# A pointwise product computed as two groups of two column blocks, with neighbouring steps moved inside it

## The chip, the cores and the metric

The kernel runs on one core of one Trainium2 chip. The metric is device time in microseconds of one execution, lower is better; times are given as the median of several runs. All arithmetic is float32 in and out. The engines named below are PE (matrix products), DVE and ACT (elementwise work), POOL (a few small powers) and SP, whose queue issues the loads.

## The reference

One layer of a hybrid block on 256 tokens of width 4096: attention heads (A) and a convolution module (C) work on the same normed input, both are gated, joined and projected; then a gated embedding is added and the result is normed. Cut to what matters here:

```python
xn = rms_norm(h, norm_in_g)
proj = xn @ w_in                       # q, k, v, z_a, a_c, g_c, z_c, 2048 columns each
y_a = chunked_attention(q, k, v, rel_table)
y_a = rms_norm(y_a, attn_out_g) * silu(z_a)
# convolution module
u = a_c * sigmoid(g_c)
u = causal_depthwise_conv(u, w_dw) + b_dw
u = silu(layer_norm(u, conv_ln_g, conv_ln_b))
y_c = u @ w_pw + b_pw                  # the pointwise product, 2048 x 2048
y_c = rms_norm(y_c, conv_out_g) * silu(z_c)
h = h + concatenate([y_a, y_c]) @ w_out
gate = sigmoid(rms_norm(h, ple_norm_g) @ w_ple_gate + b_ple_gate)
h = h + gate * (p @ w_ple)
return rms_norm(h, final_g)
```

## The kernel before

**Products.** The 256 tokens are two halves of 128 rows; an output column block is 512 wide (NB). Every float32 operand is split into a high and a low part (wh, wl for weights), and a product of two blocks is three matmuls of 128 x 512: high times wh, low times wh, high times wl. A weight tile of 128 x 1024 is loaded by SP into `wt` (5 buffers), cast to `wh` by ACT (L304, 5 buffers), and `wl` is the difference, made by DVE (L321, 5 buffers). `prepare` issues load and cast of the next unit of a plan one step ahead.

There are two forms of product. `product` (matmuls at L255) computes one column block: two accumulators (one per half of the rows) out of four PSUM banks, so that consecutive blocks alternate between two pairs of banks. `mixed_product` (matmuls at L449) computes two column blocks at once in all four banks, over 16 (or 8) pairs of 128-row weight blocks. A pair of an order is plain (8 products, 24 matmuls) or starred, which means that it is done with 7 products (21 matmuls) on sums of blocks: the weights' sums are made on DVE (L324, L327) and the inputs' sums, the combinations, lie ready in `xS`. Four further banks (acc_P) hold helper sums in such a group. Orders are strings of pair numbers; two of them matter here:

```python
    dense = units("1 0* 3 2* 5 4* 6* 7 8* 9 10* 11 12* 14* 13 15")
    delayed = units("1 3 5 7 0* 9 2* 11 4* 13 6* 15 8* 10 12 14")
```

In the first and the last pair of a `mixed_product` the matmuls go bank by bank, in between block by block.

**What runs beside the products.** Two queues of small steps are emptied inside the products: `later` (taps of the convolution, the layer norm's steps) by `fill(n)`, n steps per unit, and `closing` (the steps of heads), one step per `fill`. A scheduler then fixes one order of instructions on each engine; ACT, DVE and SP work through theirs in order.

**Around the change.** The last `heads` call queues the layer norm (`layer_norm_swish`) and computes the last v product. Of the layer norm's tail, for each of four column blocks, `swish` scales (DVE, L843) and applies the swish (ACT, L844), and `split` makes the high part (ACT, L854) and the low part (DVE, L855) of `uS`, the pointwise product's input. Then `fill(1e9)` and `finish_steps` empty both queues: the rest of the tail, v's evacuation (ACT, L953), the last heads' values (PE, L961 to L963, evacuated by ACT at L965), the squares of y_a (ACT, L564) and `r_a`. Then the scratch pool is closed and another opened; four `product` calls (32 units) compute the pointwise product, DVE adds the bias row (L1028, rows loaded at L1010) and ACT sums squares. Behind them in the program stand the eight combinations of the input (`combine_again`, six DVE instructions and one ACT copy each), whose results the four gate groups (`gated`, each a `mixed_product` over `w_in`) read. `gate_order` gives the first gate group the order `delayed` and the other three `dense`.

Of the kernel before, what the change touches and what calls it, by code (L numbers as in the profile page):

```python
# [16 lines left out]
P = 128  # L17
# [14 lines left out]
def hybrid_block(  # L32
# [40 lines left out]
    def pool(name, bufs, stack=ctx, side=0, **kw):  # L73
        return stack.enter_context(tc.tile_pool(name=name, bufs=bufs, side=sides[side], **kw))
# [83 lines left out]
    def big_tile(pool=None):  # L158
        return (pool or big).tile([P, 4, 2, T], F32R, tag="big", name="big_t")
# [45 lines left out]
    def finish_steps():  # L205
        while closing:
            step()

    def fill(n):
        step()  # L210
        credit[0] += n
        while later and credit[0] > 0:
            item = later.popleft()
            weight, item = item if isinstance(item, tuple) else (1, item)
            credit[0] -= weight
            item()
        if not later:
            credit[0] = 0
# [42 lines left out]
    def units(text):  # L261

        return [(int(u.rstrip("*")), u.endswith("*")) for u in text.split()]
# [4 lines left out]
    delayed = units("1 3 5 7 0* 9 2* 11 4* 13 6* 15 8* 10 12 14")  # L268
    early = units("1 3 5 0* 7 9 2* 11 4* 13 6* 15 8* 12 10* 14")
    late = units("1 3 5 7 9 11 13 15 0* 2 4* 6 8* 10* 12 14")  # L270

    plan, prepared = deque(), []

# [40 lines left out]
    def plan_product(w, col, kblocks, first=0):  # L314
        plan.extend((w, col, None, k0, "one") for k0 in range(first, kblocks, KC))

    def plan_pairs(w, col, apart, order):
        plan.extend((w, col, apart, pair, "seven" if seven else "pair") for pair, seven in order)
# [57 lines left out]
    def sum_rows():  # L376
        return [spool.tile([P, NB], F32, tag="row", name="comb", bufs=3) for _ in range(2)]
# [22 lines left out]
    def combine_again(dst, at, t, i, rows):  # L400

        a, s = rows
        nc.vector.tensor_tensor(
            a.rearrange("q (i t) -> q i t", t=T), t[:, i : i + 2, 0, :].bitcast(F32),
            t[:, i : i + 2, 1, :].bitcast(F32), ALU.add,
        )
        combined_parts(dst, at, s, a[:, :T], a[:, T : T + P], a[:, T + P :], 1.0)

    def comb_tile(combs):

        if len(combs) < D // NB // 2 - 1:
            combs.append(big_tile(more))
        else:
            combs.append(spool.tile([P, 4, 2, T], F32R, tag="comb", name="comb_t", bufs=1))
# [147 lines left out]
    def square_sum(dst, src):  # L562
        junk = spool.tile([P, NB], mybir.dt.bfloat16, tag="s", name="junk", bufs=1 if more_scratch else 2)
        nc.scalar.activation(junk, src, AF.Square, accum_out=dst)  # L564

    def rstd_of(partial, n, name):
        r = cpool.tile([P, partial.shape[1]], F32, name=name)
        nc.vector.tensor_reduce(r, partial, AX.X, ALU.add)
        rsqrt(r, r, n)
        return r  # L570
# [86 lines left out]
    AG_ORDER, QK_ORDER = early, early  # L657

    def gate_order(c0):
        return dense if c0 else delayed  # L660

    plan_product(w_in0, o_g, KD, FIRST)
    plan_product(w_in0, o_a, KD)
    for g in range(n_g):
# [1 line left out]
            plan_pairs(w_in0, o_a + (g + 1) * NB, o_g - o_a, AG_ORDER)  # L666
        plan_pairs(w_in0, o_q + g * NB, o_k - o_q, QK_ORDER)
        plan_product(w_in0, o_v + g * NB, KD)
    for c in range(CW // NB):
        plan_product(w_pw0, c * NB, KCW)  # L670
    for o_z in (o_za, o_zc):
        for c0 in range(0, AW // NB, 2):
            plan_pairs(w_in0, o_z + c0 * NB, NB, gate_order(o_z != o_za or c0))
# [103 lines left out]
    def layer_norm_swish():  # L777

        add = nc.vector.tensor_tensor
        st = {}  # L780

        def scratch(name):
            t = more.tile([P, 2, 4, T], F32, tag="big", name=name)
            return [t[:, j] for j in range(2)]

        def fold(s):
            add(s[:, :2, :], s[:, :2, :], s[:, 2:, :], ALU.add)
            add(s[:, 0, :], s[:, 0, :], s[:, 1, :], ALU.add)
            return s[:, 0, :]

        def stat(key, m, scale=1.0):
            st[key] = cpool.tile([P, T], F32, tag="ln_stat", name=key)
            nc.scalar.activation(st[key], m, AF.Identity, scale=scale)

        def mean(s):

            m = tmp_psum()
            nc.tensor.matmul(m[:, :T], mean_w, fold(s), start=True, stop=True)
            stat("mu", m[:, :T])

        def total(c):
            if c == 0:
                st["s"] = act.tile([P, 4, T], F32, tag="act", name="lnsum")
                add(st["s"], conv[0], conv[1], ALU.add)
            elif c > 1:
                add(st["s"], st["s"], conv[c], ALU.add)

        def center(c, i):
            cv = conv[c]
            nc.vector.tensor_tensor(cv[:, i, :], cv[:, i, :], st["mu"], ALU.subtract)  # L810

        def square(c):
            if c == 0:
                st["q"], st["t"] = scratch("sq")
            s = st["t"] if c else st["q"]
            nc.scalar.activation(s, conv[c], AF.Square)
            if c:
                add(st["q"], st["q"], s, ALU.add)

        def variance(s):  # L820

            s = fold(s)
            m = tmp_psum()
            for h in range(NH):
                nc.tensor.matmul(
                    m[:, h : h + 1], s[:, h * P : (h + 1) * P], mean_w[:, :1],
                    start=True, stop=True,
                )
            st["r"] = cpool.tile([P, NH], F32, name="r_ln")
            rsqrt(st["r"], m[:, :NH], 1)  # L830

        def spread(s):

            m = tmp_psum()
            for h in range(NH):
                d = s[:, 0, h * P : (h + 1) * P]
                nc.vector.tensor_scalar(d, ident, st["r"][:, h : h + 1], None, ALU.mult)
                nc.tensor.matmul(m[:, h * P : (h + 1) * P], mean_w, d, start=True, stop=True)
            stat("rs", m[:, :T], float(CW))

        def swish(c, i):
            cv, b = conv[c], 4 * c + i
            nc.vector.tensor_tensor(cv[:, i, :], cv[:, i, :], st["rs"], ALU.mult)  # L843
            nc.scalar.activation(  # L844
                cv[:, i, :], cv[:, i, :], AF.Silu,
                scale=ln_g[:, b : b + 1], bias=ln_b[:, b : b + 1],
            )

        def split(c, i):
            if i == 0:  # L850
                assert more is not None
                uS.append(big_tile(more))
            hi, lo = uS[c][:, i, 0, :], uS[c][:, i, 1, :]
            nc.scalar.copy(hi, conv[c][:, i, :])  # L854
            nc.vector.tensor_tensor(lo, conv[c][:, i, :], hi.bitcast(F32), ALU.subtract)  # L855

        n = len(conv)
        rest = [lambda: None] * 4
        later.extend(partial(total, c) for c in range(n))
        later.append(lambda: mean(st["s"]))  # L860
        later.extend(rest)

        def second():
            for c in range(n):
                later.extend(partial(center, c, i) for i in range(4))
                later.append(partial(square, c))
            later.append(lambda: variance(st["q"]))
            later.extend(rest)
            later.append(lambda: spread(st["t"]))
            later.extend(rest)  # L870
            for c in range(n):
                later.extend(partial(swish, c, i) for i in range(4))
            for c in range(n):
                later.extend(partial(split, c, i) for i in range(4))

        return second
# [127 lines left out]
    closing.append(lambda: r_as.append(rstd_of(ssq_a, AW, "r_a")))  # L1004


    def broadcast_row(src, n0, n):

        t = spool.tile([P, n], F32, tag="row", name="row", bufs=3)
        nc.sync.dma_start(  # L1010
            t, bass.AP(tensor=src.tensor, offset=src.offset + n0, ap=[[0, P], [1, n]])
        )
        return t

    fill(1e9)
    finish_steps()
    r_a, = r_as
    first_scratch.close()
    spool = upool = pool("lpool", 2, side=1)
    more_scratch.append(1)  # L1020
    y_c = []
    ssq_c = cpool.tile([P, NH, CW // NB], F32, name="ssq_c")
    for c in range(CW // NB):
        row = broadcast_row(b_pw, c * NB, NB)
        acc = product(w_pw0, c * NB, uS, KCW)
        y = act.tile([P, NH, NB], F32, tag="act", name="y_c")
        for h in range(NH):
            nc.vector.tensor_tensor(y[:, h, :], acc[h], row, ALU.add)  # L1028
            square_sum(ssq_c[:, h, c : c + 1], y[:, h, :])
        y_c.append(y)  # L1030
    r_c = rstd_of(ssq_c, CW, "r_c")


    xS = []
    for c in range(D // NB):
        if c % 2 == 0:
            comb_tile(xS)
        combine_again(xS[c // 2], 2 * (c % 2), xT[c], 0, sum_rows())

    def gated(ys, c0, col, r_y, order):  # L1040

# [196 lines left out]
```

## Time and profile before

| what | value |
|---|---|
| median of 3 runs | 2045.38 us (2044.98 to 2045.83) |
| the profiled execution | 2045.17 us, span 2043.4 us |
| mean granted clock of PE | 0.996 |
| layer norm's last scalings on DVE begin | 888.27 us |
| last matmul of the last v product begins | 897.87 us |
| pointwise product on PE | 901.07 to 995.85 us |
| first gate group on PE | 995.85 to 1079.50 us |
| second, third, fourth gate group | 81.60 us each |

Times inside the span are counted from its start. A row of the profile names a line of the kernel, an engine, an operation, the tile written and the tiles read; in brackets stands the idle time of the engine just before and what ended it. The span is the time from the first to the last instruction; the execution's own time is 1.8 us more.

### The profile page before, as it was taken

The numbers are of one execution on the slowest core, as the hardware profiler recorded it, in microseconds if no ns is written. First come the engines' busy times: TensorE is split into PE (matmuls) and PEld (weight loads), VectorE is DVE, ScalarE is ACT, GpSimd is POOL, SyncE is SP. The second block draws the span as 40 slices with busy tenths as digits, with TensorE's granted clock in tenths as the row PEclk, the third lists the DMA queues.
The fourth block names the chain that finished last, engine by engine and source line by source line (L and its number), as shares of the span: only waits on it lengthen the run. The fifth ranks groups of instructions, "written<-read, shape, count | busy, mean of one in ns | idle before, by whom it ended". The sixth has DMA issues, their size and how long they took to land.

```text
span 2043.4 us, 26018 instructions
## 1 busy us (share of the span) xinstructions
PE 2018.3 (99%) x9103; PEld 1668.4 (82%) x9103; DVE 1801.0 (88%) x2124; ACT 1373.3 (67%) x2033; POOL 14.7 (1%) x23
## 2 busy tenths in 40 slices
PE   9999999999999999999999999999999999999997
PEld 6888888888888888878888888888888888888886
DVE  7589997999799988975889999999999998999954
ACT  7477798778977797774555656675565675665543
POOL 0000000000000000000000000000000000000010
PEclk9999999999999999999999999999999999999999
DMA  8646665666566665746565665666656655666774
GB/s 303 186 165 207 191 208 171 213 195 208 165 198 203 196 196 175 217 153 214 171 227 173 214 208 192 239 227 198 214 191 221 206 191 191 211 229 206 230 221 144
DMA packets 170333, 412.29 MB, mean 202 GB/s; under 512 B 13006, under 2 KB 16222, under 8 KB 170202
## 3 DMA queue, kind: packets, MB, share of 16 engines
q1 hardware_dynamic: 169914, 410.11, 62.1%
q8 instruction: 71, 1.16, 0.2%
q10 hardware_dynamic: 288, 0.52, 0.1%
q14 instruction: 60, 0.49, 0.1%
HBM read 406.39 MB, written 4.19 MB: 201 GB/s over the span
## 4 chain that ended last, share of the span: by engine, by line
PE 95%; DVE 2%; ACT 1%; issue 1%; DMA 1%; ACTq 0%; POOLq 0%; POOL 0%; DVEq 0%
PE acc L449 55%; PE acc L255 22%; PE acc_P L449 15%; DVE wl L321 1%; PE tmp_ps L179 1%; DMA wt<-in_w_in_dram 0%; PE tmp_ps L888 0%; PE tmp_ps L924 0%; PE tmp_ps L946 0%; ACT big_t L854 0%; ACT wh L304 0%; ACT junk L564 0%; PE tmp_ps L134 0%; DMA pin<-in_p_dram 0%; PE tmp_ps L923 0%
## 5 line engine op out<-in xcount | busy, mean ns | idle before, releaser
L321 DVE TENSOR_TENSOR wl<-wt,wh 128x1024 fp32r<-128x1024 f32 x961 | 1091.8, 1156 | 143.0 <-ACT wh L304 119.4
L449 PE MATMUL acc<-wh,big_t 128*128 128x512 f32 x3410 | 1052.2, 390 | 1.3 <-ACT big_t L165 0.7
L304 ACT CAST wh<-wt 128x1024 fp32r<-128x1024 f32 x727 | 698.5, 981 | 324.1 <-PE acc L449 106.1
L449 PEld LDWEIGHTS acc<-wh,big_t 128*128 128x128 f32 x3410 | 638.4, 188 | 133.5 <-ACT big_t L165 1.2
L449 PE MATMUL acc<-wl,big_t 128*128 128x512 f32 x1705 | 662.8, 389 | 0.4 <-DVE wl L321 0.4
L255 PE MATMUL acc<-wh,big_t 128*128 128x512 f32 x1248 | 393.8, 397 | 7.1 <-ACT wh L304 5.7
L449 PEld LDWEIGHTS acc<-wl,big_t 128*128 128x128 f32 x1705 | 320.0, 188 | 67.5 <-DVE wl L321 0.8
L255 PEld LDWEIGHTS acc<-wh,big_t 128*128 128x128 f32 x1248 | 232.5, 189 | 55.8 <-ACT wh L304 6.5
L449 PE MATMUL acc_P<-wh,big_t 128*128 128x512 f32 x852 | 262.2, 389 | 0.3 <-ACT wh L491 0.3
L255 PE MATMUL acc<-wl,big_t 128*128 128x512 f32 x624 | 244.1, 392 | 0.1
L327 DVE TENSOR_TENSOR wt<-wt 128x512 f32<-128x512 f32 x234 | 224.2, 958 | 7.5
L491 ACT CAST wh<-wt 128x1024 fp32r<-128x1024 f32 x117 | 123.3, 1054 | 158.1 <-DVE wt L327 129.2
L716 ACT ACTIVATE prod<-uT,dw 128x255 f32<-128x255 f32 (+14 forms) x480 | 200.7, 489 | 2.7 <-DVE cv L723 2.5
L449 PEld LDWEIGHTS acc_P<-wh,big_t 128*128 128x128 f32 x852 | 159.7, 188 | 33.6 <-ACT wh L491 0.7
L488 ACT CAST wh<-wt 128x1024 fp32r<-128x1024 f32 x117 | 123.3, 1054 | 81.5 <-DVE wt L327 76.4
L449 PE MATMUL acc_P<-wl,big_t 128*128 128x512 f32 x426 | 165.3, 389 | 0.0
L723 DVE TENSOR_TENSOR cv<-cv,prod 128x1020 f32<-128x1020 f32 (+14 forms) x120 | 138.7, 1156 | 21.2 <-ACT prod L716 21.0
L255 PEld LDWEIGHTS acc<-wl,big_t 128*128 128x128 f32 x624 | 117.5, 189 | 26.5 <-DVE wl L321 1.3
L449 PEld LDWEIGHTS acc_P<-wl,big_t 128*128 128x128 f32 x426 | 79.9, 188 | 17.0 <-DVE wl L321 0.2
L324 DVE TENSOR_TENSOR wt<-wt 128x512 f32<-128x512 f32 x117 | 80.2, 685 | 0.2 <-DMA wt<-in_w_ple_gate_dram 0.2
L564 ACT ACTIVATE junk<-hc 128x512 bf16<-128x512 f32 x32 | 20.2, 630 | 20.9 <-DVE hc L1095 8.4
L165 ACT ACTIVATE big_t<-tmp_ps,prm 128x256 fp32r<-128x256 f32 x64 | 27.5, 473 | 4.6 <-DVE big_t L166 4.6
(190 smaller groups left out, 937.9 us busy)
## 6 DMA issues: line engine op xcount, KB each, us to landing
wt<-in_w_in_dram SPq DMA_DIRECT2D x447, 512.0 KB, 4.6
wt<-in_w_out_dram SPq DMA_DIRECT2D x128, 512.0 KB, 4.6
wt<-in_w_ple_gate_dram SPq DMA_DIRECT2D x128, 512.0 KB, 4.4
wt<-in_w_pw_dram SPq DMA_DIRECT2D x32, 512.0 KB, 4.6
hc<-in_x_dram SPq DMA_DIRECT2D x8, 512.0 KB, 5.4
wt<-in_w_ple_dram SPq DMA_DIRECT2D x8, 512.0 KB, 5.5
out_dram<-hc SPq DMA_DIRECT2D x16, 256.0 KB, 2.7
xin<-in_x_dram SPq DMA_DIRECT2D x7, 512.0 KB, 8.0
```

The lines of the kernel that those rows point to most:

```text
L165: nc.scalar.activation(hi, src, AF.Identity, scale=scale),
L179: nc.tensor.transpose(pt[:, i * T + h * P : i * T + (h + 1) * P], src[:, h, b * P : (b + 1) * P], ident,)
L255: nc.tensor.matmul(acc, a, b[:, k, :], start=kb == 0 and kind == 0, stop=kb == kblocks - 1 and kind == 2,)
L304: chain(nc.scalar.copy(highs[k][:, :n], wt[:, :n]))
L321: return chain(nc.vector.tensor_tensor(wl, wt, wh.bitcast(F32), ALU.subtract))
L324: return chain(nc.vector.tensor_tensor(out, a, b, ALU.add))
L327: return chain(nc.vector.tensor_tensor(out, a, b, ALU.subtract))
L449: nc.tensor.matmul(banks[name], a, b, start=name not in begun, stop=final and ends[name] == n and kind == 2,)
L488: chain(nc.scalar.copy(ah, w0))
L491: chain(nc.scalar.copy(bh, w1))
L716: chain(nc.scalar.activation(dst[:, i, : T - n], uT[:, i, : T - n], AF.Identity, scale=dw[:, b, TAPS - 1 - n : TAPS - n], bias=0.0 if n el ...
L723: chain(nc.vector.tensor_tensor(cv[:, :, n:], cv[:, :, n:], made[n][:, :, : T - n], ALU.add))
```

## The change

Three things are rearranged; what is computed stays the same.

- The pointwise product becomes two `mixed_product` calls, each of two column blocks in four banks, over eight plain pairs (`plain8`). Its loads are 128 rows of 1024 columns in place of two blocks of 128 x 512.
- `swish` and `split` are queued column block by column block. Before the product only the steps up to column block 0 are emptied; the other 24 are emptied inside the first group, 4 per pair, and so are v's evacuation, the values, the squares, `r_a` and the change of scratch pools, which are now `closing` steps.
- The combinations become `later` steps of the second group, one per pair. All four gate groups take the order `dense`.

```diff
+    plain8 = units(" ".join(str(i) for i in range(KCW // 2)))
...
     def gate_order(c0):
-        return dense if c0 else delayed
+        return dense
...
-    for c in range(CW // NB):
-        plan_product(w_pw0, c * NB, KCW)
+    for c0 in range(0, CW // NB, 2):
+        plan_pairs(w_pw0, c0 * NB, NB, plain8)
...
             for c in range(n):
                 later.extend(partial(swish, c, i) for i in range(4))
-            for c in range(n):
                 later.extend(partial(split, c, i) for i in range(4))
...
-    fill(1e9)
-    finish_steps()
-    r_a, = r_as
-    first_scratch.close()
-    spool = upool = pool("lpool", 2, side=1)
-    more_scratch.append(1)
+    while len(later) > 8 * (CW // NB - 1):
+        later.popleft()()
+
+    def next_scratch():
+        nonlocal spool, upool
+        first_scratch.close()
+        spool = upool = pool("lpool", 2, side=1)
+        more_scratch.append(1)
+
+    closing.append(next_scratch)
+    xS = []
+
+    def comb_x(c):
+        if c == 0:
+            xS.append(spool.tile([P, 4, 2, T], F32R, tag="comb", name="comb_t", bufs=1))
+        elif c % 2 == 0:
+            xS.append(big_tile(more))
+        combine_again(xS[c // 2], 2 * (c % 2), xT[c], 0, sum_rows())
+
     y_c = []
     ssq_c = cpool.tile([P, NH, CW // NB], F32, name="ssq_c")
-    for c in range(CW // NB):
-        row = broadcast_row(b_pw, c * NB, NB)
-        acc = product(w_pw0, c * NB, uS, KCW)
-        y = act.tile([P, NH, NB], F32, tag="act", name="y_c")
-        for h in range(NH):
-            nc.vector.tensor_tensor(y[:, h, :], acc[h], row, ALU.add)
-            square_sum(ssq_c[:, h, c : c + 1], y[:, h, :])
-        y_c.append(y)
+    for c0 in range(0, CW // NB, 2):
+        acc = mixed_product(w_pw0, c0 * NB, uS, None, plain8, None, fills=4 if c0 == 0 else 1)
+        if c0 == 0:
+            fill(1e9)
+            finish_steps()
+            later.extend(partial(comb_x, c) for c in range(D // NB))
+        ys = [act.tile([P, NH, NB], F32, tag="act", name="y_c") for _ in range(2)]
+        rows = [broadcast_row(b_pw, (c0 + j) * NB, NB, "brow") for j in range(2)]
+        for h, j in QUARTERS:
+            tt(ys[j][:, h, :], acc[h][j], rows[j], ALU.add)
+            square_sum(ssq_c[:, h, c0 + j : c0 + j + 1], ys[j][:, h, :])
+        y_c.extend(ys)
+    r_a, = r_as
     r_c = rstd_of(ssq_c, CW, "r_c")
-
-
-    xS = []
-    for c in range(D // NB):
-        if c % 2 == 0:
-            comb_tile(xS)
-        combine_again(xS[c // 2], 2 * (c % 2), xT[c], 0, sum_rows())
+    fill(1e9)
```

How the change moves instructions is read from the order on each engine. On ACT, from the end of the layer norm on, before (cv: the convolution's output; big_t: a tile of `uS`; acc_7590 and acc_7591: the last v product; x15: so many in a row):

```order
L844 ACT_TABLE_LOAD
L844 ACTIVATE cv<-cv,prm 128x256 x15
L953 ACTIVATE v<-acc_7590,r_x 128x512
L953 ACTIVATE v<-acc_7591,r_x 128x512
L844 ACTIVATE cv<-cv,prm 128x256
L854 CAST big_t<-cv 128x256 x16
L965 ACTIVATE y_a<-tmp_ps,den 128x128 x8
L564 ACTIVATE junk,ssq_a<-y_a 128x512 x2
L304 CAST wh<-wt 128x1024 x12
```

and now, at the same place (lines are two further down):

```order
L846 ACT_TABLE_LOAD
L846 ACTIVATE cv<-cv,prm 128x256 x4
L856 CAST big_t<-cv 128x256 x4
L846 ACTIVATE cv<-cv,prm 128x256
L306 CAST wh<-wt 128x1024
L846 ACTIVATE cv<-cv,prm 128x256 x3
L856 CAST big_t<-cv 128x256
L306 CAST wh<-wt 128x1024 x2
L954 ACTIVATE v<-acc_7590,r_x 128x512
L954 ACTIVATE v<-acc_7591,r_x 128x512
L856 CAST big_t<-cv 128x256 x3
L846 ACTIVATE cv<-cv,prm 128x256
```

The weight casts of the pointwise product (wh; the one of its first tile stands ahead of these rows in both orders) now stand between the swishes and ahead of v's evacuation, where all 12 stood behind the squares. On DVE at the same place, before:

```order
L843 TENSOR_TENSOR cv<-cv,rs 128x256 x16
L321 TENSOR_TENSOR wl<-wt,wh 128x1024
L855 TENSOR_TENSOR big_t<-cv,big_t 128x256 x16
L568 TENSOR_REDUCE r_a<-ssq_a 128x2
L147 TENSOR_SCALAR r_a<-r_a 128x2
L321 TENSOR_TENSOR wl<-wt,wh 128x1024 x11
```

and now:

```order
L845 TENSOR_TENSOR cv<-cv,rs 128x256 x8
L323 TENSOR_TENSOR wl<-wt,wh 128x1024
L845 TENSOR_TENSOR cv<-cv,rs 128x256 x2
L857 TENSOR_TENSOR big_t<-cv,big_t 128x256 x4
L845 TENSOR_TENSOR cv<-cv,rs 128x256 x3
L323 TENSOR_TENSOR wl<-wt,wh 128x1024
L845 TENSOR_TENSOR cv<-cv,rs 128x256 x2
L857 TENSOR_TENSOR big_t<-cv,big_t 128x256
```

Here the 16 scalings and 16 low parts, two blocks before, are cut up, with the low weight parts (wl) of the first tiles between them. Where the first group of the new product hands its four banks (acc_8081 to acc_8084) to the second, DVE has now:

```order
L390 SCALAR_TENSOR_TENSOR comb<-comb 128x128
L405 TENSOR_TENSOR comb<-big_t 128x512
L323 TENSOR_TENSOR wl<-wt,wh 128x1024 x5
L1046 TENSOR_TENSOR y_c<-acc_8081,row 128x512
L1046 TENSOR_TENSOR y_c<-acc_8083,row 128x512
L1046 TENSOR_TENSOR y_c<-acc_8082,row 128x512
L1046 TENSOR_TENSOR y_c<-acc_8084,row 128x512
L323 TENSOR_TENSOR wl<-wt,wh 128x1024 x6
```

The additions that empty the four banks stand together, with five low weight parts ahead of them and combinations (comb) already begun in the first group; before, two such additions stood between 8 or more low weight parts. On SP the first two bias rows now stand behind 14 of the product's weight loads, where three rows stood behind 6.

More of the change, by code (lines that the diff above doesn't have):

```diff
@@ L1004, in hybrid_block, with broadcast_row @@
     closing.append(lambda: r_as.append(rstd_of(ssq_a, AW, "r_a")))
-    def broadcast_row(src, n0, n):
-        t = spool.tile([P, n], F32, tag="row", name="row", bufs=3)
+    def broadcast_row(src, n0, n, tag="row"):
+        t = spool.tile([P, n], F32, tag=tag, name="row", bufs=3 if tag == "row" else 2)
         nc.sync.dma_start(
```

## The prediction

> **What bounds the kernel now.** I read the page's busy times first, then its chain that ended last.
>
> ```profile
> span 2043.4 us, 26018 instructions
> PE 2018.3 (99%) x9103; PEld 1668.4 (82%) x9103; DVE 1801.0 (88%) x2124; ACT 1373.3 (67%) x2033; POOL 14.7 (1%) x23
> PE 95%; DVE 2%; ACT 1%; issue 1%; DMA 1%; ACTq 0%; POOLq 0%; POOL 0%; DVEq 0%
> ```
>
> PE (the matrix engine) is busy 99% of the span and holds 95% of the chain. A busy PE need not be at its peak, so I took its pace from the timeline of PE inside the pointwise product.
>
> ```profile
> 914.77 0.62 PE L255 MATMUL acc<-wh,big_t 128*128 128x512 f32 x2
> ...
> 933.13 0.62 PE L255 MATMUL acc<-wh,big_t 128*128 128x512 f32 x2
> ```
>
> Between these two rows stand 27 repeats of "two matmuls with wh, one with wl", 81 matmuls in 18.36 us: **0.2267 us each**. A plain pair of weight blocks (24 matmuls) thus takes 5.44 us of PE. So only two things can change the time: how many matmuls there are, and where PE stands still or runs slowly. The list of what PE waited for, over the whole span, has one long entry; the other row quoted is all that the four-bank products (L449) ever waited for the low weight parts:
>
> ```profile
> PE acc L255 <- ACT wh L304: 5.7, 2, 4.5
> PE acc L449 <- DVE wl L321: 0.4, 1, 0.4
> ```
>
> The 4.5 us wait stands exactly where the change is made. The PE timeline there, and the granted clock of three stretches:
>
> ```profile
> 897.87 0.39 PE L255 MATMUL acc<-wl,big_t 128*128 128x512 f32 x1
> 898.36 0.49 PE L961 MATMUL tmp_ps<-v,pT 128*128 128x128 f32 x2
> ...
> 901.07 0.71 PE L255 MATMUL acc<-wh,big_t 128*128 128x512 f32 x2
> ...
> 903.70 0.39 PE L255 MATMUL acc<-wl,big_t 128*128 128x512 f32 x1
> 908.62 1.22 PE L255 MATMUL acc<-wh,big_t 128*128 128x512 f32 x2 [4.54 <-ACT wh L304]
> 903.93:908.62 4.69, 0.15 (x1) 0.00 (x0) 1.67 (x7) 4.69 (x16) 0.50 (x1) 0.82 0.00 0
> 908.62:914.08 5.46, 5.42 (x12) 3.83 (x13) 5.46 (x5) 3.74 (x4) 0.18 (x1) 0.53 0.86 260
> 914.08:919.52 5.44, 5.44 (x25) 4.50 (x24) 2.11 (x3) 2.12 (x3) 0.00 (x0) 1.00 0.97 311
> ```
>
> (In a row of the stretches, the fields after the length are busy time of PE, weight load, DVE, ACT, POOL, then granted clock, DMA share and GB/s.) The last value product ends at 897.87 + 0.23 = 898.10. The 24 small value matmuls and the first pointwise step (12 matmuls) run; from 903.93 PE stands for 4.69 us; the next 12 matmuls take 5.46 us instead of 12 x 0.2267 = 2.72, at a granted clock of 0.53; from 914.08 all is normal. The chain of waits says who held PE:
>
> ```profile
> 897.62 1.37 ACT v L953 x2
> 898.98 0.49 ACT cv L844
> 899.47 4.90 ACT big_t L854 x16
> 904.37 2.05 ACT y_a L965 x8
> ...
> 907.64 0.94 ACT wh L304
> ```
>
> ACT's queue is in order: behind v it does all 16 high parts of the layer norm's output, the last heads' y_a and its squares, and only then the weight casts (wh) that PE needs.
>
> **The change, part by part.** (1) *The stop.* ACT and DVE durations from their timelines:
>
> ```profile
> 888.27 5.46 DVE L843 TENSOR_TENSOR cv<-cv,rs 128x256 f32<-128x256 f32 x16
> 908.60 5.77 DVE L321 TENSOR_TENSOR wl<-wt,wh 128x1024 fp32r<-128x1024 f32 x5 [0.57 <-ACT wh L304]
> 889.55 7.51 ACT L844 ACTIVATE cv<-cv,prm 128x256 f32<-128x256 f32 x15
> 907.51 4.85 ACT L304 CAST wh<-wt 128x1024 fp32r<-128x1024 f32 x5
> ```
>
> Per instruction: scaling 0.34, low weight part 1.15, swish 0.50, weight cast 0.97; a high part 4.90/16 = 0.31, and a low part of the output I take as 0.34 like the scaling (same shape). Up to 888 us the engines' orders are the old ones. In the new order ACT does 4 swishes, 4 high parts, 1 swish, and then the cast of the second weight tile: 889.55 + 2.00 + 1.23 + 0.50 + 0.97 = 894.3. DVE does 8 scalings, a low weight part, 2 scalings (888.27 + 2.7 + 1.15 + 0.7 = 892.8), 4 low parts (894.2), 3 scalings (895.2), the second tile's low part: 896.4. PE reaches the first pair at 898.10 and wants that last one at its sixth matmul, 899.2. So the first pair starts without a wait, with **2.9 us to spare**. Casts three and four now stand ahead of v's evacuation: they end at 898.0, v at 899.3; the third of the four banks, which v frees, is wanted after 12 matmuls, 900.8. The value matmuls come in two halves behind pairs one and two, at 903.5 and 910.3, when v is long there. Column block 1 is wanted at 911.7; its last high part stands 11 ACT instructions behind 894.3 in the order, done at 894.3 + 1.5 + 0.3 + 1.9 + 1.4 + 0.9 = 900.3. Later pairs have more room: a cast is allowed as soon as its buffer of five is free, some 10.9 us (four half pairs of 2.72) ahead of its use.
>
> So PE does 898.10 to 914.08 worth of work (24 matmuls x 0.2267 = 5.44, and the value matmuls' 901.07 - 898.36 = 2.71) in 8.15 us in place of 15.98: **-7.83 us**. If the small matmuls cost up to 0.4 us more by being split, or 0.7 less, that is in the range.
>
> (2) *Fewer matmuls.* The first gate group takes the order "dense" (8 starred pairs) in place of "delayed" (5). A starred pair has 7 products of 3 matmuls, a plain one 8: 3 x 3 = 9 matmuls fewer, x 0.2267 = **-2.04 us**. The trace has both orders:
>
> ```profile
> 898.10:914.08 15.98, 11.30 (x49) 8.69 (x49) 11.27 (x23) 14.26 (x36) 0.69 (x1) 0.79 0.29 89
> 914.08:995.85 81.77, 81.77 (x362) 67.72 (x361) 50.94 (x65) 38.12 (x47) 0.00 (x0) 1.00 0.68 214
> 995.85:1079.50 83.65, 83.65 (x371) 69.27 (x370) 72.21 (x92) 46.22 (x54) 1.67 (x1) 1.00 0.61 195
> 1079.50:1161.10 81.60, 81.60 (x361) 67.57 (x361) 77.79 (x84) 49.23 (x55) 0.00 (x0) 1.00 0.63 206
> ```
>
> The third row is the first gate group, the fourth the second one: 83.65 - 81.60 = 2.05. DVE pays: by the order it gets 6 more 128x1024 and 9 more 128x512 instructions, 6 x 1.22 + 9 x 0.69 = 13.5 us. From 898.10 to 1079.50 it is busy 11.27 + 50.94 + 72.21 = 134.4; with 13.5 more, 147.9 of 171.5 us, 86%. That hides it; if it all fell into the gate group, the second group's 77.79 of 81.60 shows that it still fits.
>
> (3) *Two groups of four banks.* The 384 matmuls stay 384. Each group's four banks are emptied by four DVE additions, 0.69 each by this row:
>
> ```profile
> 929.93 1.37 DVE L1028 TENSOR_TENSOR y_c<-acc,row 128x512 f32<-128x512 f32 x2
> ```
>
> The last pair is computed bank by bank, so the first bank is finished 18 matmuls (4.08 us) before the next group wants it. Queued behind these additions on DVE are the low weight parts from the fourth tile of the next group on, which PE wants 8.2 us into it. Cost 0 while DVE is under 4.08 - 0.69 = 3.4 us late.
>
> (4) *Moved combinations.* They go from the product's end into its two groups: 0 added. Three of the four result tiles reuse the product's input tiles; the last comes free after pair six of the second group, 898.10 + 2.71 + 14 x 5.44 = 977.0, leaving 993.3 - 977.0 = 16 us for two casts and two low parts of under 0.7 each before the first starred pair. The weight casts behind them on ACT wait for that same pair anyway.
>
> (5) *Queues of the DMAs.* SP issues the first two bias rows behind 14 weight loads (6 before); they wait until the old scratch is read, which by the sums ends with the squares near 914. The load behind them is wanted at 898.10 + 2.71 + 7 x 5.44 = 938.9 and lands in 4.6 us (below): nothing lost.
>
> ```profile
> wt<-in_w_pw_dram SPq DMA_DIRECT2D x32, 512.0 KB, 4.6
> ```
>
> **Sum.** The profiled execution took 2045.17 us (span 2043.4 plus 1.8 around it): 2045.17 - 7.83 - 2.04 = **2035.3**. The median of the three runs is 0.21 higher, so I predict 2035.4 us, 0.49% faster.
>
> **The rivals.** *A rest of the stop stays.* The margin of 2.9 us rests on a sum over 19 DVE instructions. If DVE or ACT is 3 us later than that margin allows, PE waits 3 us: 2038.3; the full 4.69, with the slow 12 matmuls (5.46 - 2.72 = 2.74), would give 7.43 back: 2042.7. For it: both engines are in order. Against it: the sums. The Trainium skill ("TensorE: Matmul & The Clock Gate", "Part 1: The HAM clock gate") has the clock halved only after an idle window of about 3.4 us; the 4.69 us stop with its 0.53 agrees, and by it a rest of 3 us costs just itself.
>
> *DVE becomes the bound in the first gate group.* Then the 9 matmuls bring nothing: 2045.17 - 7.83 = 2037.3. Against it: DVE at 77.79 of 81.60 in the next group, with PE unbroken.
>
> *Slower: both new hand-overs stop PE.* The place is the first matmul of the second group and of the first gate group. If DVE reaches the emptying 8.1 us late (3.4 + 4.69) at each, PE stops twice as it did at 903.93: 2 x 7.43 = 14.9, and 2035.3 + 14.9 = 2050.2. Before, two of the four banks were free at such a moment. For it: in the new order five low weight parts stand ahead of the emptying. Against it: the fifth needs a buffer that PE frees 5.44 us before the group's end, so it ends 5.44 - 0.97 - 1.15 = 3.3 us before it, and the four emptyings follow PE; and the gate groups do the same hand-over with 81.60 of 81.60 busy.
>
> *Four banks in turn keep the clock low.* The Trainium skill ("TensorE: Matmul & The Clock Gate", "A second HAM failure mode: psum-queue depth-cycling") tells of a kernel whose PE, cycling through banks, idled so often that its clock swung. Here that would put the product's 384 matmuls (87.1 us) at the 0.79 of the row 898.10:914.08: 23 us more, 2058. The gate groups cycle through four banks and more at 1.00.
>
> *The change doesn't do what it says*: ACT's order or the waits leave the stop, and only the matmuls count: 2043.1. The new orders above speak against it.
>
> **How the numbers follow.** Forecast 0.80; rest of the stop 0.08; DVE bound 0.04; hand-overs 0.03; clock 0.01; no effect on the stop 0.04. The range takes the 0.7 us that the small matmuls may gain and a rest of up to 4 us: 2034.0 to 2039.5. About 0.2% (4.1 us) can be told from no change: faster 0.91, same 0.05, slower 0.04.
>
> **What would show it.** Right: the wait of 4.5 us gone from PE's list, granted clock 1.00 from 898 to 920, first gate group at 81.6 us, 9 matmuls fewer. Wrong: PE waits at the first pointwise pair (step 1), at the group ends near 944 or 988 (step 3), or in the first gate group (step 2), for DVE or ACT.

## The result, and the profile after

The changed kernel takes **2034.99 us** (median of 4 runs, 2034.51 to 2035.89); the kernel before, run beside it, 2045.59 us (4 runs, 2044.98 to 2045.83). The ratio is 0.9949, with a 95% interval of 0.9932 to 0.9966: 0.5% faster. The profiled execution took 2035.35 us; the sum of the prediction had 2035.3 for it.

The page of the kernel after: span, busy times, and the shares of the chain that ended last.

```profile
span 2033.6 us, 26040 instructions
PE 2013.0 (99%) x9094; PEld 1665.1 (82%) x9094; DVE 1812.8 (89%) x2139; ACT 1379.0 (68%) x2039; POOL 13.9 (1%) x23
PE 95%; DVE 2%; issue 1%; ACT 1%; DMA 1%; ACTq 0%; POOLq 0%; POOL 0%; DVEq 0%
```

PE still bounds the kernel, with 9 matmuls fewer (9094 for 9103). In the list of what PE waited for, the entry that held the stop (5.7 us in all, 4.5 the longest, before) now reads:

```profile
PE acc L255 <- ACT wh L306: 1.1, 1, 1.1
```

None is left for the product, whose matmuls are now those of L451. In the timeline of PE at the start of the pointwise product (start, duration, engine, line, operation, tiles) the stop is gone:

```profile
898.01 0.39 PE L255 MATMUL acc<-wl,big_t 128*128 128x512 f32 x1
898.23 0.61 PE L451 MATMUL acc<-wh,big_t 128*128 128x512 f32 x2
...
903.67 0.38 PE L962 MATMUL tmp_ps<-v,pT 128*128 128x128 f32 x2
...
904.93 0.71 PE L451 MATMUL acc<-wh,big_t 128*128 128x512 f32 x2
...
910.47 0.38 PE L962 MATMUL tmp_ps<-v,pT 128*128 128x128 f32 x2
...
911.72 0.71 PE L451 MATMUL acc<-wh,big_t 128*128 128x512 f32 x2
```

The first pointwise matmul follows the last of the v product at once, without a wait in brackets. The value matmuls stand in two halves, 1.26 and 1.25 us long. Three stretches of the kernel after (length, busy time of PE, weight load, DVE, ACT, POOL, granted clock, DMA share, GB/s):

```profile
898.10:914.08 15.98, 15.98 (x84) 13.66 (x83) 10.46 (x14) 15.57 (x35) 0.00 (x0) 1.00 0.70 220
987.85:1069.45 81.60, 81.60 (x362) 67.57 (x361) 76.36 (x82) 49.27 (x57) 0.69 (x1) 1.00 0.61 206
898.10:1069.45 171.35, 171.35 (x770) 142.32 (x769) 141.70 (x185) 101.92 (x142) 1.49 (x2) 1.00 0.63 205
```

The first row is the stretch that held the stop: 84 matmuls at clock 1.00, where 49 stood at 0.79. The second is the first gate group, now as long as the other three. The third runs from the product to that group's end: PE is never idle, and DVE is idle for 30 of the 171 us.

From the timelines of ACT and DVE, the instructions that feed the first pairs:

```profile
893.40 1.05 ACT L306 CAST wh<-wt 128x1024 fp32r<-128x1024 f32 x1
...
898.03 1.26 ACT L954 ACTIVATE v<-acc,r_x 128x512 f32<-128x512 f32 x2
899.18 1.02 ACT L856 CAST big_t<-cv 128x256 fp32r<-128x256 f32 x3
895.25 1.22 DVE L323 TENSOR_TENSOR wl<-wt,wh 128x1024 fp32r<-128x1024 f32 x1
```

The cast of the second weight tile ends at 894.45, v is evacuated at 899.29, column block 1's high parts are done at 900.20, and the second tile's low part at 896.47: PE wants that last one only with its sixth matmul of the product, which starts at 899.37.

### The profile page after: what moved, and what is told of

Its sections match the earlier page's. It is cut to its first block, busy times and chain, and to the rows that moved or that the text cites. A ratio compares the mean times of both kernels' runs of the same rounds, so it can differ in the third digit from the quotient of the medians.

```text
span 2033.6 us, 26040 instructions
## 1 busy us (share of the span) xinstructions
PE 2013.0 (99%) x9094; PEld 1665.1 (82%) x9094; DVE 1812.8 (89%) x2139; ACT 1379.0 (68%) x2039; POOL 13.9 (1%) x23
## 4 chain that ended last, share of the span: by engine, by line
PE 95%; DVE 2%; issue 1%; ACT 1%; DMA 1%; ACTq 0%; POOLq 0%; POOL 0%; DVEq 0%
PE acc L451 59%; PE acc L255 17%; PE acc_P L451 16%; DVE wl L323 1%; PE tmp_ps L179 1%; DMA wt<-in_w_in_dram 0%; PE tmp_ps L889 0%; PE tmp_ps L925 0%; PE tmp_ps L947 0%; DMA pin<-in_p_dram 0%; ACT wh L306 0%; PE tmp_ps L134 0%; PE tmp_ps L963 0%; PE tmp_ps L964 0%; PE tmp_ps L962 0%
## 5 line engine op out<-in xcount | busy, mean ns | idle before, releaser
L451 PE MATMUL acc<-wh,big_t 128*128 128x512 f32 x3632 | 1120.7, 390 | 1.2 <-DVE big_t L166 0.6
L451 PEld LDWEIGHTS acc<-wh,big_t 128*128 128x128 f32 x3632 | 679.7, 188 | 142.1 <-DVE big_t L166 1.0
L451 PE MATMUL acc<-wl,big_t 128*128 128x512 f32 x1816 | 705.9, 389 | 0.4 <-DVE wl L323 0.4
L451 PEld LDWEIGHTS acc<-wl,big_t 128*128 128x128 f32 x1816 | 340.8, 188 | 71.7 <-DVE wl L323 0.9
L451 PE MATMUL acc_P<-wh,big_t 128*128 128x512 f32 x864 | 265.9, 389 | 0.3 <-ACT wh L493 0.3
L329 DVE TENSOR_TENSOR wt<-wt 128x512 f32<-128x512 f32 x240 | 230.0, 958 | 7.6
L451 PEld LDWEIGHTS acc_P<-wh,big_t 128*128 128x128 f32 x864 | 161.9, 188 | 34.1 <-ACT wh L493 0.7
L451 PE MATMUL acc_P<-wl,big_t 128*128 128x512 f32 x432 | 167.6, 389 | 0.0
L451 PEld LDWEIGHTS acc_P<-wl,big_t 128*128 128x128 f32 x432 | 81.0, 188 | 17.0
L326 DVE TENSOR_TENSOR wt<-wt 128x512 f32<-128x512 f32 x120 | 82.4, 686 | 1.2 <-DMA wt<-in_w_in_dram 1.2
L166 DVE SCALAR_TENSOR_TENSOR big_t<-tmp_ps,prm,big_t 128x256 fp32r<-128x256 f32 x64 | 28.8, 480 | 2.3 <-ACT big_t L165 2.3
```

The source lines that it names most:

```text
L166: nc.vector.scalar_tensor_tensor(lo, src, scale, hi.bitcast(F32), ALU.mult, ALU.subtract),
L326: return chain(nc.vector.tensor_tensor(out, a, b, ALU.add))
L329: return chain(nc.vector.tensor_tensor(out, a, b, ALU.subtract))
L451: nc.tensor.matmul(banks[name], a, b, start=name not in begun, stop=final and ends[name] == n and kind == 2,)
```

## The experiments

All lines below are those of the changed kernel. Times are medians; where a difference to 2034.99 us is given, it is a difference of medians.

**1. The gate order back.** Is the second term of the sum there, and how large?

```diff
-        return dense
+        return dense if c0 else delayed
```

> The changed kernel with one thing undone: the first gate group gets its old order, delayed (5 starred pairs). My theory (the nine matmuls count on their own, 0.2267 us each): 2.04 us above the changed kernel's 2035.0, so 2037.0, the first gate group 83.65 us long, no wait of PE at the pointwise product. Rival (DVE was the bound of that group anyway, the order brings nothing): 2035.0.

Measured: 2037.54 us (2036.03 to 2038.65), ratio to before 0.9960 (0.9945 to 0.9975). So the dense order is worth 2.55 us in the changed kernel by the medians; 9 matmuls at 0.2267 make 2.04, and the runs of this kernel scatter by more than the difference. PE does not wait at the product, and 83.65 us from the start of the first gate group on hold 371 matmuls without a wait, as many as before. The profile shows where some of the scatter comes from. One stretch at the start of the kernel, far from the change, first in this kernel and then in the changed one:

```profile
18.86:22.27 3.41, 3.41 (x12) 2.73 (x12) 2.87 (x5) 2.68 (x7) 0.00 (x0) 0.50 1.06 377
18.86:22.27 3.41, 3.41 (x19) 2.74 (x19) 3.31 (x6) 3.41 (x9) 0.00 (x0) 1.00 1.05 375
```

Just ahead of it PE stands still in both, for 1.53 us here (17.05 to 18.58) and 1.52 us there (17.15 to 18.67). Here the clock is halved behind that stop, there it is not. To the same point of its work PE then needs 3.76 us (18.58 to 22.34) instead of 2.32 (18.67 to 20.99): 1.44 us of this execution's 2038.65 have nothing to do with the order.

**2. The dense order alone,** in the kernel before, with nothing else changed.

```diff
-        return dense if c0 else delayed
+        return dense
```

> The kernel before with one thing of the change alone: all gate groups get the order dense. Theory A (with the combinations still at the product's end, DVE is late for the first two starred pairs; summed along its order, PE waits 0.3 + 1.4 + 1.5 us): the nine matmuls' 2.04 us are lost again and 1.2 more, 2046.8. Theory B (the five buffers absorb it): 2045.6 - 2.04 = 2043.55.

Measured: 2045.50 us, ratio 1.0002 (0.9992 to 1.0012): nothing gained. The longest of the new entries in the list of what PE waited for in this kernel (its lines are numbered as in the kernel before):

```profile
PE acc_P L449 <- ACT wh L491: 1.4, 3, 0.7
```

Two of the three waits in PE's timeline:

```profile
1015.00 0.73 PE L449 MATMUL acc_P<-wh,big_t 128*128 128x512 f32 x2 [0.33 <-ACT wh L491]
1031.21 0.50 PE L449 MATMUL acc_P<-wh,big_t 128*128 128x512 f32 x1 [0.73 <-ACT wh L491]
```

And the stretch of the first gate group:

```profile
995.85:1079.50 83.65, 82.59 (x362) 67.35 (x361) 82.62 (x106) 50.92 (x60) 9.83 (x1) 1.00 0.60 201
```

Read this row against the same stretch of before: 83.65 us again, with 362 matmuls where 371 stood. DVE is busy 82.62 of 83.65 us, since the combinations (done before at the product's end and in this group) and the extra weight sums of the denser order fall together; the casts of those sums (L491, which wait for DVE) come late. The 9 matmuls were taken out, and waiting for DVE took the time back. Neither theory had it: the time is neither longer, as by A, nor shorter, as by B. In the changed kernel, with the combinations moved into the product, DVE is at 76.36 of 81.60 us in that group, and PE has no wait. No run moves the combinations alone, so that it is they that make the room is read from these loads.

**3. Nothing emptied inside the product.** The layer norm's tail, the values, the squares and `r_a` go ahead of it again; the two groups of four banks, the moved combinations and the dense order stay.

```diff
-    closing.append(next_scratch)
+    fill(1e9)
+    finish_steps()
+    next_scratch()
```

> The changed kernel, but the layer norm's tail, the last values, the squares and r_a are all emptied before the pointwise product, as they were before; the two groups of four banks stay. My theory (ACT's order makes the stop): the third weight cast stands behind all swishes, high parts, y_a and squares and ends near 909.9; PE is out of work near 906.6, so it stops for about 3.3 us, and up to 2.7 us more if its clock drops: 2038.3 to 2041. Rival 1 (the two-group form alone removes the stop): 2035.0. Rival 2 (the whole old loss of 7.83 comes back): 2042.8.

Measured: 2040.02 us (8 runs, 2037.76 to 2041.15), ratio 0.9971 (0.9961 to 0.9982): 5.03 us of the gain gone. The timeline of this kernel, three rows of ACT and then two of PE:

```profile
893.52 1.03 ACT L306 CAST wh<-wt 128x1024 fp32r<-128x1024 f32 x1
...
905.55 2.14 ACT L966 ACTIVATE y_a<-tmp_ps,den 128x128 f32<-128x128 f32 x8
...
908.80 4.85 ACT L306 CAST wh<-wt 128x1024 fp32r<-128x1024 f32 x5
906.41 0.39 PE L451 MATMUL acc<-wl,big_t 128*128 128x512 f32 x1
909.91 1.94 PE L451 MATMUL acc<-wh,big_t 128*128 128x512 f32 x6 [3.11 <-ACT wh L306]
```

And the whole stretch at half clock behind the stop:

```profile
911.10:914.51 3.41, 3.41 (x10) 2.64 (x9) 3.41 (x5) 2.55 (x3) 0.00 (x0) 0.50 0.67 214
```

The casts, from the third tile's on, stand behind the tail and the squares again, and PE stands still from 906.41 + 0.23 = 906.64 to 909.91: 3.27 us. Then the clock is halved for 3.4 us, and the 12 matmuls from 909.91 to 914.21 take 4.30 us instead of 2.72, which with a little at the edge is 1.7 more. 3.27 + 1.7 = 5.0, the difference of the medians. So what is emptied ahead of the product makes this stop, and moving it inside removes it.

The old stop does not come back whole, though. Before, it began at 903.93, after 12 matmuls of the product, and lasted 4.69 us; here it begins after 24 and lasts 3.27. A unit of `mixed_product` has two weight tiles, one of `product` has one, and `prepare` casts one unit ahead: the cast of the second tile (893.52) now stands ahead of v. Stop and slow stretch together cost 3.27 + 1.58 = 4.85 us, where before they cost 4.69 + 2.74 = 7.43. Some 2.6 us of the old loss is thus gone with the steps still ahead; that it is the two-group form which does this is read from the kernel and this order, and was not run by itself in the kernel before.

**4. Four single blocks, with the same interleaving.** The product in the old form, four calls of one column block each, with all steps inside the first block and the combinations from the second one on.

```diff
-        plan_pairs(w_pw0, c0 * NB, NB, plain8)
+        plan_product(w_pw0, c * NB, KCW)
...
-        acc = mixed_product(w_pw0, c0 * NB, uS, None, plain8, None, fills=4 if c0 == 0 else 1)
+        acc = product(w_pw0, c * NB, uS, KCW, fills=4 if c == 0 else 1)
```

> The pointwise product as four single column blocks again (two banks each), but with the tail and the heads' last steps inside its first block and the combinations inside the others, and dense in all gate groups. My theory (the interleaving removes the stop, not the two-group form): no wait at the product's start; the combinations come later, which may cost DVE up to 1.5 us in the first gate group: 2035.0 to 2036.5. Rival (one block uses up the layer norm's output in half the time, so the tail is late): PE waits 2 us or more inside the first block, 2037 to 2040.

Measured: 2035.68 us (5 runs, 2034.35 to 2037.36), ratio 0.9956 (0.9941 to 0.9971). The stretch of the whole product in this kernel:

```profile
898.10:988.00 89.90, 89.90 (x410) 74.87 (x410) 64.32 (x101) 53.14 (x83) 0.79 (x1) 1.00 0.65 205
```

PE has no idle moment in it, and the first gate group behind it takes 81.60 us without a wait, so the later combinations cost nothing either. Once the steps stand inside the first block, the two-group form adds nothing that these runs can tell.

**5. How much may stand ahead of the product.** Steps of two, then of three column blocks of the tail are emptied ahead, instead of one.

```diff
-    while len(later) > 8 * (CW // NB - 1):
+    while len(later) > 8 * (CW // NB - 2):
```

> The changed kernel with two column blocks of the tail emptied before the product. By the order on ACT, v is evacuated by 899.6 and 900.2, its banks are wanted at 900.8 and 902.2: no wait, 2035.0. Rival (the margins that I summed do not hold): 0.5 to 2 us more.

> The changed kernel with three column blocks of the layer norm's tail emptied before the product in place of one. By the order on ACT, the evacuation of v moves behind eight more swishes and high parts and ends its first half near 902.8; the third bank is wanted at 900.8. My theory: PE waits about 2.0 us there for ACT's v, and its clock does not drop (the stop is short): 2037.0. Rival (there is more room than summed): 2035.0. Rival (any stop lowers the clock): 2037.0 plus about 2.7.

Measured: with two blocks 2034.80 us (ratio 0.9947, 0.9930 to 0.9964), with three 2036.40 us (2035.02 to 2037.07; ratio 0.9954, 0.9939 to 0.9969). PE's timeline with three:

```profile
901.83 0.39 PE L451 MATMUL acc<-wl,big_t 128*128 128x512 f32 x1
902.47 1.20 PE L451 MATMUL acc<-wh,big_t 128*128 128x512 f32 x4 [0.25 <-ACT wh L306]
903.73 0.73 PE L451 MATMUL acc<-wl,big_t 128*128 128x512 f32 x2
904.30 0.62 PE L451 MATMUL acc<-wh,big_t 128*128 128x512 f32 x2
```

From 901.83 to 904.30 stand 7 matmuls in 2.47 us instead of 1.59, so 0.88 us of the 1.4 lost is here, in short waits; the rest is within the scatter of the runs. The casts of the third and fourth weight tile on ACT, first in the changed kernel and then with three blocks:

```profile
896.13 2.01 ACT L306 CAST wh<-wt 128x1024 fp32r<-128x1024 f32 x2
901.37 2.00 ACT L306 CAST wh<-wt 128x1024 fp32r<-128x1024 f32 x2
```

PE's first matmul of the product starts at 898.23 in the changed kernel, at 897.82 with two blocks and at 899.34 with three; the two casts, which begin at 896.65 with two blocks, begin 2.1 us before it, 1.2 us before it and 2.0 us behind it. So a second block moves little: the scheduler had put its swishes and its first high part ahead of these casts already, and only three high parts (0.9 us) are new there. That costs nothing. A third block adds 3.2 us of ACT (a swish of 4 takes 2.0, a high part of 4 takes 1.2), and these casts come too late. It is for the third cast that PE waits by the row, and not for v, as I had expected: v is evacuated only from 903.27 on, when PE is at work again. My 2.0 us of wait was too much as well.

**6. DVE made late at the hand-over.** The rival on the slower side needs DVE late when the first group hands its banks to the second. Extra additions on DVE, which read the first bank again and write a part of `y_c` that the kernel's own addition then overwrites, make it late by a known amount: 4 and 12 of them.

```diff
         for h, j in QUARTERS:
             tt(ys[j][:, h, :], acc[h][j], rows[j], ALU.add)
+            for _ in range(12 if (c0, h, j) == (0, 0, 0) else 0):
+                tt(ys[0][:, 1, :], acc[0][0], rows[0], ALU.add)
```

> The changed kernel with four extra additions of 128x512 on DVE (the first bank of group one added to its row again, into a place that is overwritten later) before the first bank is given free. Theory (the hand-over has some 3 us of room): by DVE's order the bank comes free near 945.9, it is wanted at 944.5, and the second at 947.6: PE waits 1.5 to 2.0 us, clock not lowered, 2036.7. Rival (the hand-over has no room): 4 x 0.6 = 2.4 and more. Rival (it hides all): 2035.0.

> The same with twelve extra additions. Theory: the bank comes free near 953.0 by DVE's order, PE stops for about 8.5 us and then runs 12 matmuls at half clock (2.7 us): 2035.0 + 11.2 = 2046.2, slower than the kernel before. Rival (no loss by the clock): 2043.5.

Measured: with 4 additions 2034.69 us (ratio 0.9950, 0.9934 to 0.9966), all hidden; with 12, 2039.14 us (7 runs, 2037.24 to 2040.01; ratio 0.9970, 0.9958 to 0.9981), 4.15 us lost and not 11. DVE at the hand-over, first in the changed kernel, where no addition is extra:

```profile
941.22 1.41 DVE L1046 TENSOR_TENSOR y_c<-acc,row 128x512 f32<-128x512 f32 x2
943.30 0.69 DVE L1046 TENSOR_TENSOR y_c<-acc,row 128x512 f32<-128x512 f32 x1 [0.67 <-PE acc L451]
944.66 0.69 DVE L1046 TENSOR_TENSOR y_c<-acc,row 128x512 f32<-128x512 f32 x1 [0.67 <-PE acc L451]
945.27 2.36 DVE L323 TENSOR_TENSOR wl<-wt,wh 128x1024 fp32r<-128x1024 f32 x2
950.28 2.36 DVE L323 TENSOR_TENSOR wl<-wt,wh 128x1024 fp32r<-128x1024 f32 x2 [2.65 <-ACT wh L306]
```

and then DVE and PE in the kernel with 12:

```profile
948.46 5.03 DVE L1048 TENSOR_TENSOR y_c<-acc,row 128x512 f32<-128x512 f32 x7
950.76 0.39 PE L451 MATMUL acc<-wl,big_t 128*128 128x512 f32 x1
953.55 0.73 PE L451 MATMUL acc<-wh,big_t 128*128 128x512 f32 x2 [2.40 <-DVE y_c L1048]
```

The stretch at half clock behind its stop:

```profile
954.57:957.99 3.42, 3.42 (x10) 2.63 (x9) 0.40 (x1) 2.67 (x6) 0.00 (x0) 0.50 0.22 77
```

In the changed kernel DVE waits for PE at the hand-over (0.67 us twice) and for ACT soon after (2.65 us), so DVE has idle time there, 4.0 us, for 4 more additions of 0.72. With 12 it frees the first bank at 953.49, and PE stands from 950.99 to 953.55, 2.56 us. My sums were wrong in what PE does meanwhile. The program's scheduler, which knows of the additions, lets PE do 30 matmuls of the second group (944.19 to 950.99) before it needs the held bank: 30 x 0.2267 = 6.8 us of cover in place of the 3.4 I had counted. Behind the stop the clock falls to half; the 12 matmuls from 953.55 to 957.98 lose 4.43 - 2.72 = 1.71, and 2.56 + 1.71 = 4.27 answers to the measured 4.15.

**7. From which length does a stop slow the clock?** The same with 10, 11 and 14 additions (the 12 in the diff above), since experiments 3 and 6 showed a slow stretch behind stops of 3.27 and 2.56 us, for which the prediction had charged the stop alone.

> 10 extra additions (two fewer than 12, each 0.72 us): DVE frees the held bank 1.4 us earlier, so the stop of PE, 2.56 us with 12 (950.99 to 953.55), is 1.1 us. Theory 1, only a stop of about 2.5 us or more halves PE's clock afterwards: just the stop, 2034.99 + 1.1 = 2036.1 us, granted clock 1.00 throughout. Theory 2, a stop of any length does: 1.1 + 1.7 (the lost time after the stop with 12) = 2037.8 us and a stretch of some 3 us at 0.5 behind it.

> 11 extra additions: the stop of PE is 2.56 - 0.72 = 1.8 us. Theory 1 (only from about 2.5 us on): 2034.99 + 1.8 = 2036.8 us, clock 1.00 behind it. Theory 2 (any length): 1.8 + 1.7 more, 2038.5 us, with some 3 us at 0.5.

> 14 extra additions: the stop of PE is 2.56 + 2 x 0.72 = 4.0 us. Both theories: the clock halves, and costs 1.7 (as with 12) to 2.7 us (as before the change, behind 4.69 us): 2034.99 + 4.0 + 1.7 to 2.7 = 2040.7 to 2041.7 us. If only a whole idle window of 3.4 us did it, this run alone of the late ones would show it, and the run with 12 would be a chance.

Where PE resumes in the kernel with 10 additions, by its timeline:

```profile
952.19 0.73 PE L451 MATMUL acc<-wh,big_t 128*128 128x512 f32 x2 [0.94 <-DVE y_c L1048]
```

In the kernel with 11, the same row, and below it the stretch from 957 to 960 with its granted clock:

```profile
952.47 0.73 PE L451 MATMUL acc<-wh,big_t 128*128 128x512 f32 x2 [1.67 <-DVE y_c L1048]
957.00:960.00 3.00, 3.00 (x15) 2.49 (x14) 2.73 (x3) 2.94 (x5) 0.00 (x0) 1.00 0.60 183
```

And both in the kernel with 14:

```profile
954.55 0.74 PE L451 MATMUL acc<-wh,big_t 128*128 128x512 f32 x2 [3.85 <-DVE y_c L1048]
957.00:960.00 3.00, 3.00 (x10) 2.37 (x9) 1.48 (x2) 2.54 (x4) 0.00 (x0) 0.61 0.12 40
```

| additions | stop of PE (us) | lowest clock behind it | median (us) | more than 2034.99 | ratio to before |
|---|---|---|---|---|---|
| 10 | 1.10 | 1.00 | 2035.65 | 0.66 | 0.9950 (0.9934 to 0.9967) |
| 11 | 1.83 | 1.00 | 2036.59 | 1.60 | 0.9956 (0.9941 to 0.9971) |
| 12 | 2.56 | 0.50 | 2039.14 | 4.15 | 0.9970 (0.9958 to 0.9981) |
| 14 | 4.00 | 0.50 | 2041.18 | 6.19 | 0.9980 (0.9971 to 0.9990) |

(The stop is counted from the last matmul's start plus 0.23 to the next one's start.) The run with 14 came out as expected. Theory 2, that a stop of any length halves the clock, is out: stops of 1.10 and 1.83 us cost about themselves, and from 11 to 12 additions, 0.72 us more on DVE, the time rises by 2.55 us. Theory 1 fits these four profiles, one for each length, but the length alone does not decide: in experiment 1 the clock fell behind a stop of 1.53 us in one execution, and behind the same stop in the changed kernel it did not. The runs with 12 spread from 2037.24, which is the stop alone (2034.99 + 2.56 = 2037.55), to 2040.01: whether that length halves the clock seems to differ from one execution to the next. The runs with 14 fall into two groups too (2040.41 to 2040.66 and 2041.70 to 2042.32), and one run of experiment 3, at 2037.76, has no more than its stop (2034.99 + 3.27 = 2038.26). Only one run of each has a profile, so that reading is not shown for these stops.

## Why the prediction was right

**Step 1, the stop.** Right in mechanism and nearly in size. Four points of time that it rested on came out as summed: the second tile's low part at 896.47 (896.4 predicted), v at 899.29 (899.3), column block 1's high parts at 900.20 (900.3), and the first pair without a wait. The sum had 8.15 us for 24 matmuls and the value matmuls; the two halves of the latter took 1.26 + 1.25 = 2.51 instead of 2.71, so the step brought about 8.0 and not 7.83. Experiment 3 shows the cause: with the steps ahead again a stop for the weight casts returns. The 2.9 us of room came out too: 899.37 - 896.47. What the account of the step left out is that two changes bear on the old stop: the two-group form, which casts two tiles ahead, seems to take 2.6 us of its price away by itself (experiment 3), and the interleaving takes all of it, with that form or without (experiment 4). The sum counts the whole once, so its figure is not touched.

**Step 2, fewer matmuls.** The first gate group takes 81.60 us as computed, and experiment 1 gives 2.55 for the 2.04, within its scatter. DVE's load from 898 to the group's end was estimated at 147.9 us and is 141.70. What the prediction undervalued is why DVE has room: it treated the denser order and the moved combinations as two edits, the one worth 2.04 and the other 0. Experiment 2 shows that in the kernel before, where the combinations still stand at the product's end and inside that group, the order brings nothing. That DVE becomes the bound in the first gate group, a rival at 0.04, is what happens in that kernel.

**Step 3, two groups of four banks.** Cost 0, as predicted: the fifth low weight part ended at 941.31 (940.08 + 1.23), 3.15 us before PE's end of the group at 944.46 (3.3 predicted), and the additions followed PE:

```profile
940.08 1.23 DVE L323 TENSOR_TENSOR wl<-wt,wh 128x1024 fp32r<-128x1024 f32 x1 [1.50 <-ACT wh L306]
```

Experiment 4 adds that the form is no gain beside the interleaving. The room of 3.4 us was too small, and with it the point from which the slower rival decides: it took 10 additions, some 7 us of DVE, to stop PE for 1.1.

**Steps 4 and 5, combinations and queues.** No wait of PE stands in either, from 898.10 to 1069.45; they were not tested apart from the rest, but for experiment 2.

**The sum.** 2045.17 - 8.0 - 2.04 = 2035.1 beside 2035.35 in the profiled execution; the last 0.2 us are less than runs of one kernel differ.

**The rivals.** No rest of the stop stayed, and four banks in turn did not slow the clock: it is 1.00 in every row of the product. Here the tale of the Trainium skill ("TensorE: Matmul & The Clock Gate", "A second HAM failure mode: psum-queue depth-cycling") doesn't apply, as PE never idles between banks.

**What was wrong.** The sentence in the rivals that a rest of 3 us "costs just itself". It leaned on the Trainium skill ("TensorE: Matmul & The Clock Gate", "Part 1: The HAM clock gate"), by which the clock falls after an idle window of about 3.4 us. Stops of 2.56 and 3.27 us halved it as well in the profiled executions, for 1.7 us more each. The measurement decides: by an estimate from these two, a rest of 3 us would have come out near 2040, not 2038.3. The range, which reached to 2039.5, was too narrow on this side; its lower end, 2034.0, is 0.6 us below what the working gives (2035.3 - 0.7). The forecast itself rested on neither.

## What to carry to other kernels

Where a profile of a matmul-bound kernel has one long wait, read backwards through the in-order queue of the engine that ends it: what stands ahead there and isn't needed yet can be cut into pieces and put behind the first few things that PE needs. Here that was enough, and the room for it could be summed instruction by instruction to some tenths of a microsecond. Fewer matmuls are worth their time only where the engine that prepares them has room in that very stretch, so weigh such an edit together with the one that makes the room. Price a stop of PE by its length, and allow for a slow clock behind it, which cost some 1.7 us here: it followed all profiled stops from 2.56 us on, and once a stop of 1.53 us.

## What the hardware showed that was not expected

- The clock fell to 0.50 behind stops of 2.56, 3.27, 4.00 and 4.69 us, not behind 1.10 and 1.83; behind a stop of 1.53 us at the kernel's start it fell in experiment 1, and behind the same stop of 1.52 us in the changed kernel it did not. What decides between executions stays open.
- The stretches at half clock lasted 3.41 us (experiments 1, 3, 6 and, with 14 additions, 955.94 to 959.35) or twice that, as in the kernel before:

```profile
906.95:913.78 6.83, 5.12 (x11) 3.62 (x12) 5.51 (x7) 5.41 (x8) 0.69 (x1) 0.50 0.65 195
```

The length of 3.41 us agrees with the window of about 3.4 us that the Trainium skill gives ("TensorE: Matmul & The Clock Gate", "Part 1: The HAM clock gate"); that a stop shorter than the window suffices does not follow from what it says there.

- The price of the slow stretch was 1.7 us behind the stops of 2.56 and 3.27 us, half of its 3.41 us: it began 1.0 and 1.2 us after PE had resumed, so PE was at work all through it. In the kernel before, the clock fell at 906.95, inside the stop, and some 5.2 of the 6.83 us lay behind the stop, which cost 2.74.
